# Rotary embedding on split heads: all transfers on one queue in one fixed order

## The chip, the cores and the metric

The kernel runs on one core of a Trainium2 chip. The metric is device time in microseconds (us); the time before is the median of three runs. Times inside the run are from one profiled execution and count from its first instruction. Sizes such as 2048 KB are in units of 1024 bytes, as the profile gives them; MB and GB/s are decimal.

## What is computed

Each of 16 heads of 64 elements is rotated by tables `cos` and `sin` that depend on the position in the sequence:

```python
batch, seq, dim = (16, 512, 1024)      # float32, num_heads = 16
x = x.reshape(batch, seq, num_heads, head_dim)
x1, x2 = (x[..., :half_dim], x[..., half_dim:])
cos = cos[None, :, None, :]; sin = sin[None, :, None, :]
rotated = np.concatenate([x1 * cos - x2 * sin, x1 * sin + x2 * cos], axis=-1)
```

So 33.55 MB are read and 33.55 MB are written. All arithmetic is in float32.

## The kernel before

**Tiles.** Each batch is 512 rows of 1024 values, which is 4 rows on each of 128 partitions (2048 KB). The first two and the last two batches are moved one at a time (single tiles, 2048 KB); the twelve between them are moved as six pairs (pair tiles, 4096 KB, 8 rows to a partition). That makes ten tiles: 0 and 1 single, 2 to 7 pairs, 8 and 9 single. This text calls the load of tile t Lt and its store St. A "row" below is one 128x1024 piece, so there are 64 of them.

**The ring.** `x_sb` holds 40 rows. The work is done in place: a tile is loaded into the ring, its rows are overwritten by the results, and the store reads from there. Tiles 0 to 5 fill the ring. Tile 6 takes the place of tiles 0 and 1, tile 7 that of tile 2, tiles 8 and 9 that of tile 3; so L6 must wait until S0 and S1 have landed, L7 until S2, and L8 and L9 until S3 (`sem_out`).

**Compute.** For a row, VectorE multiplies by cos into PSUM (`t1_ps`, L293), and GpSimd multiplies the swapped halves by the signed sin table into `t2_sb` (L257); for one row of each pair tile VectorE does that second product as well (L286). The two products are added by VectorE (L304, 43 rows), or by TensorE with an identity matrix into the same PSUM (L224), after which ScalarE copies the sum to the ring (L191, 21 rows). There are three PSUM buffers and six `t2_sb` buffers, so the engines can run apart by a few rows only. At the start ScalarE and TensorE also lay out the tables for the pair tiles.

**Transfers.** Two hardware queues are used, one for each direction. ScalarE issues the loads and the two 64 KB table transfers (L153, L174): L0, the tables, and L1 to L5 at once at the start, which fill the ring; the other four loads stand between its copies, `LAG` = 10 rows after the last row of what they overwrite, and each first waits on `sem_out`. SyncE issues the stores (L161), each as soon as the last row of its tile is added (`wait_added`). On SyncE nothing else is queued. The end of the kernel is SyncE's wait on `sem_rest` for the last stores (L162).

The order of the engines' own work is written out by hand and is the same before and after; nothing in it is decided by a scheduler.

Of the kernel before, what the change touches and what calls it, by code (L numbers as in the profile page):

```python
# [6 lines left out]
def bass_split_heads_rope_kernel(  # L7
# [21 lines left out]
    R1 = seq // P  # L29
    R2 = 2 * R1  # L30
# [10 lines left out]
    tiles = [(b, R1 if b in singles else R2) for b in range(batch) if b in singles or b % 2 == 0]  # L41
    NT = len(tiles)
    RING = 5 * R2

    rows = [(t, r) for t, (_, n) in enumerate(tiles) for r in range(n)]
    NU = len(rows)
    EARLY = (NU - RING) // R2


    V_ROW = 3  # L50
    PE2 = [R1 <= u < NU - R1 and u % R2 in (1, 3, 6) for u in range(NU)]
# [11 lines left out]
    BANK = 512  # L63
    EH = H * HD // BANK
    LEAD = 1
    LAG = 10

    with ExitStack() as stack:
        x_sb = stack.enter_context(nc.sbuf_tensor([P, RING, H, 2, HALF], fp32))
        t2_sb = stack.enter_context(nc.sbuf_tensor([P, NT2, H, 2, HALF], fp32))  # L70
        stage = stack.enter_context(nc.sbuf_tensor([P, 2, R1 * HALF], fp32))
# [9 lines left out]
        sem_out = [stack.enter_context(nc.semaphore(f"out{k}")) for k in range(EARLY)]  # L81
        sem_rest = stack.enter_context(nc.semaphore("rest"))
        sem_cos = stack.enter_context(nc.semaphore("cos"))
        sem_sin = stack.enter_context(nc.semaphore("sin"))
# [28 lines left out]
        def in_dram(single, pairs, t):  # L113
            b, n = tiles[t]
            return single[b] if n == R1 else pairs[:, b:b + 2, :]

        def in_sbuf(t):
            b, n = tiles[t]
            k = b * R1 % RING
            return x_sb[:, k:k + n].rearrange("p n h t d -> p (n h t d)")  # L120

        def where(u):
            t, r = rows[u]
            return t, r, u % RING
# [7 lines left out]
        def wait_added(eng, u):  # L132

            if n_pe[u]:
                eng.wait_ge(sem_a, n_pe[u])
            if n_comb[u]:
                eng.wait_ge(sem_v, n_comb[u])
# [10 lines left out]
        def stores_of(k):  # L148

            return sum(b * R1 // R2 == k for b, _ in tiles)  # L150

        def load(eng, t):
            eng.dma_start(in_sbuf(t), in_dram(x1, x2, t)).then_inc(sem_in[t], 16)  # L153

        def on_sync(sp):
            for u in range(NU):
                t, r, k = where(u)
                if r == tiles[t][1] - 1:
                    wait_added(sp, u)
                    k = u // R2  # L160
                    sp.dma_start(in_dram(o1, o2, t), in_sbuf(t)).then_inc(sem_out[k] if k < EARLY else sem_rest, 16)  # L161
            sp.wait_ge(sem_rest, 16 * sum(stores_of(k) for k in range(EARLY, NU // R2)))  # L162

        def on_scalar(ae):
            later = {}
            for t, (b, n) in enumerate(tiles):
                if b * R1 + n <= RING:
                    load(ae, t)
                else:

                    later.setdefault((b * R1 - RING) // R2 * R2 + R2 - 1 + LAG, []).append(t)
                if t == 0:
                    for i, (table, sem) in enumerate(((cos, sem_cos), (sin, sem_sin))):
                        ae.dma_start(stage[:, i, :], table.rearrange("(s r) d -> s (r d)", r=R1)).then_inc(sem, 16)  # L174

            ae.wait_ge(sem_i, 2)
            ae.activation(  # L177
                pick[:], ident[:].rearrange("q (s k) -> q k s", k=2)[:, :, :, None].broadcast_to([P, 2, P // 2, 2]), COPY
            ).then_inc(sem_g, 1)
            ae.wait_ge(sem_sin, 16)  # L180
            sv = stage[:, 1, :].rearrange("s (r d) -> s r d", d=HALF)
            ae.activation(s1_sb[:, :, 0, :], sv, COPY, scale=-1.0)  # L182
            ae.activation(s1_sb[:, :, 1, :], sv, COPY).then_inc(sem_s, 1)  # L183
            ae.wait_ge(sem_t, 2)
            s2 = s2_sb[:].rearrange("p (k r) t d -> p k r t d", r=R1)
            ae.activation(s2[:, :, :, 0, :], pair_ps[:, :, 1, :, :], COPY, scale=-1.0)  # L186
            ae.activation(s2[:, :, :, 1, :], pair_ps[:, :, 1, :, :], COPY).then_inc(sem_s, 1)  # L187
            for u in range(NU):
                if PE2[u]:
                    ae.wait_ge(sem_e, n_pe[u])  # L190
                    ae.activation(xs[:, u % RING, :], t1_ps[:, u % NT1, :], COPY).then_inc(sem_a, 1)  # L191
                for t in later.get(u, ()):
                    k = (tiles[t][0] * R1 - RING) // R2
                    ae.wait_ge(sem_out[k], 16 * stores_of(k))
                    load(ae, t)

        def on_tensor(pe):
            pe.wait_ge(sem_z, 1)
# [62 lines left out]
        def on_vector(ve):  # L261
# [49 lines left out]
            for u in range(NU + LEAD):  # L311
                if u < NU:
                    mul(u)
                if u >= LEAD and not PE2[u - LEAD]:
                    comb(u - LEAD)

        on_sync(nc.sync)
        on_scalar(nc.scalar)
        on_gpsimd(nc.gpsimd)
        on_tensor(nc.tensor)  # L320
# [34 lines left out]
```

## Time and profile before

| What | Before |
|---|---|
| Time, median of 3 runs (lowest to highest) | 161.23 us (161.17 to 161.33) |
| Profiled execution: span, first to last instruction | 160.3 us |
| GpSimd busy | 134.9 us (84%) |
| VectorE busy | 130.3 us (81%) |
| TensorE busy | 72.8 us (45%) |
| ScalarE busy | 24.4 us (15%) |
| Moved | 67.26 MB, mean 419 GB/s |
| Transfers | 10 loads, 10 stores, 2 tables |

How to read it: the page gives the profiled execution its span alone and no second time of its own, so the span stands for it. The median of the runs is 0.9 us more than the span; that part lies before the first or after the last instruction of the profile. Busy times add up instructions on one engine and say nothing about which wait ends last. A transfer's "time to landing" runs from its issue to the moment when its semaphore is complete, so it holds the time in which it was queued behind others.

### The profile page before, as it was taken

Reading aid. Unit: us, or ns where it says so; the run is one execution under the profiler, and the core shown is the slowest. Engines: PE = TensorE matmul, PEld = TensorE weight load, DVE = VectorE, ACT = ScalarE, POOL = GpSimd, SP = SyncE. Lnnn points to the kernel's source line nnn. Section 1 sums busy time; section 2 is a strip of 40 time slices with the busy share of each in tenths; the row PEclk is TensorE's granted clock in tenths of the full one; section 3 lists DMA queues with packets and bytes.
Section 4 is the critical chain, followed back from the end, with each engine's and each line's share of the span. In section 5 each row is a group of like instructions: output and inputs, shape, how many; then the busy total and the mean of one; then the engine's idle time right before and its main releaser. Section 6 shows DMA issues by size and latency. Waiting matters only on the chain.

```text
span 160.3 us, 522 instructions
## 1 busy us (share of the span) xinstructions
PE 72.8 (45%) x94; PEld 24.0 (15%) x94; DVE 130.3 (81%) x117; ACT 24.4 (15%) x27; POOL 134.9 (84%) x64
## 2 busy tenths in 40 slices
PE   6050004478357936660847105489458435850000
PEld 1020002022202211210221002022202111220000
DVE  0069998599989999996999709899889999999500
ACT  0420000203120222022012010201220402040000
POOL 1059999999999999999999999699999999289400
PEclk9955555557755587689687965555555977699555
DMA  5999999999999999999999999999999999999896
GB/s 147 409 441 474 409 450 409 425 429 429 446 429 458 417 411 466 409 433 401 450 433 425 425 409 458 409 433 433 411 429 462 441 417 401 450 441 441 376 450 294
DMA packets 3170, 67.26 MB, mean 419 GB/s; under 512 B 352, under 2 KB 608, under 8 KB 608
## 3 DMA queue, kind: packets, MB, share of 16 engines
q10 hardware_dynamic: 1728, 33.69, 49.6%
q1 hardware_dynamic: 1440, 33.56, 48.9%
q14 instruction: 2, 0.02, 0.0%
HBM read 33.69 MB, written 33.55 MB: 419 GB/s over the span
## 4 chain that ended last, share of the span: by engine, by line
DMA 60%; POOL 13%; DVE 8%; PE 7%; issue 3%; ACT 2%; ACTq 1%; DVEq 0%
DMA x_sb<-in_x_dram 41%; DMA out_dram<-x_sb 18%; POOL t_sb L257 13%; PE t_ps L224 7%; DVE t_ps L293 5%; DVE x_sb L304 3%; ACT x_sb L191 2%; ACTq L153 1%; ACTq L174 1%; DVE t_sb L286 0%; DVEq L303 0%
## 5 line engine op out<-in xcount | busy, mean ns | idle before, releaser
L257 POOL TENSOR_TENSOR t_sb<-x_sb,s_sb 128x1024 f32<-128x1024 f32 x58 | 134.2, 2346 | 14.8 <-ACT s_sb L183 8.5
L224 PE MATMUL t_ps<-t_sb,ident 128*128 128x512 f32 x84 | 68.0, 957 | 63.0 <-DVE t_ps L293 39.2
L293 DVE TENSOR_TENSOR t_ps<-x_sb,pair_ps 128x1024 f32<-128x1024 f32 x48 | 57.7, 1223 | 9.9 <-ACT x_sb L191 9.8
L304 DVE TENSOR_TENSOR x_sb<-t_ps,t_sb 128x1024 f32<-128x1024 f32 x43 | 52.4, 1218 | 2.6 <-POOL t_sb L257 2.6
L224 PEld LDWEIGHTS t_ps<-t_sb,ident 128*128 128x128 f32 x84 | 22.1, 290 | 108.9 <-DVE t_ps L293 74.6
L191 ACT ACTIVATE x_sb<-t_ps 128x1024 f32<-128x1024 f32 x21 | 21.5, 1023 | 109.9 <-PE t_ps L224 96.9
L293 DVE TENSOR_TENSOR t_ps<-x_sb,tab_ps 128x1024 f32<-128x1024 f32 x16 | 19.3, 1222 | 0.1
L286 DVE TENSOR_TENSOR t_sb<-x_sb,tab_ps 128x1024 f32<-128x1024 f32 x6 | 7.3, 1213 | 0.0
L264 DVE COPY tab_ps<-stage 128x128 f32<-128x128 f32 x1 | 0.3, 294 | 7.8 <-DMA stage<-in_cos_dram 7.8
L208 PE MATMUL pair_ps<-stage,pick 128*128 128x256 f32 x4 | 2.0, 667 | 5.4 <-DMA stage<-in_sin_dram 5.4
L201 PE MATMUL t_ps<-zero 128*128 128x512 bf16 x6 | 2.7, 627 | 1.3 <-DVE zero L262 1.3
L208 PEld LDWEIGHTS pair_ps<-stage,pick 128*128 128x128 f32 x4 | 1.2, 324 | 6.4 <-issue 6.3
L177 ACT ACT_TABLE_LOAD x1 | 1.3, 1283 | 5.5 <-issue 5.5
L201 PEld LDWEIGHTS t_ps<-zero 128*128 128x128 bf16 x6 | 0.7, 136 | 2.4 <-DVE zero L262 1.2
L262 DVE MEMSET zero<- 128x256 uint32 x1 | 0.3, 272 | 0.9 <-PEq L337 0.9
L186 ACT ACTIVATE s_sb<-pair_ps 128x256 f32<-128x256 f32 x1 | 0.4, 383 | 1.7 <-PE pair_ps L208 1.7
L182 ACT ACTIVATE s_sb<-stage 128x128 f32<-128x128 f32 x1 | 0.3, 309 | 2.1 <-DMA stage<-in_sin_dram 2.1
L235 POOL MEMSET ident<- 128x128 f32 x1 | 0.2, 204 | 0.3 <-POOLq L337 0.3
L177 ACT ACTIVATE pick<-ident 128x256 f32<-128x256 f32 x1 | 0.4, 416 | 0.0
L187 ACT ACTIVATE s_sb<-pair_ps 128x256 f32<-128x256 f32 x1 | 0.4, 379 | 0.0
L237 POOL TENSOR_SCALAR_AFFINE_SELECT ident<-ident 128x128 f32<-128x128 f32 x1 | 0.3, 292 | 0.1
L337 POOL MEMSET const-float32-0.0<- 128x1 f32 x1 | 0.1, 98 | 0.3 <-issue 0.3
(6 smaller groups left out, 1.0 us busy)
## 6 DMA issues: line engine op xcount, KB each, us to landing
x_sb<-in_x_dram ACTq DMA_DIRECT2D x6, 4096.0 KB, 38.0
out_dram<-x_sb SPq DMA_DIRECT2D x6, 4096.0 KB, 25.0
x_sb<-in_x_dram ACTq DMA_DIRECT2D x4, 2048.0 KB, 22.6
out_dram<-x_sb SPq DMA_DIRECT2D x4, 2048.0 KB, 15.2
stage<-in_cos_dram ACTq DMA_DIRECT2D x1, 64.0 KB, 7.8
stage<-in_sin_dram ACTq DMA_DIRECT2D x1, 64.0 KB, 7.5
```

The lines of the kernel that those rows point to most:

```text
L153: eng.dma_start(in_sbuf(t), in_dram(x1, x2, t)).then_inc(sem_in[t], 16)
L174: ae.dma_start(stage[:, i, :], table.rearrange("(s r) d -> s (r d)", r=R1)).then_inc(sem, 16)
L177: ae.activation(pick[:], ident[:].rearrange("q (s k) -> q k s", k=2)[:, :, :, None].broadcast_to([P, 2, P // 2, 2]), COPY).then_inc(sem_g, 1)
L186: ae.activation(s2[:, :, :, 0, :], pair_ps[:, :, 1, :, :], COPY, scale=-1.0)
L191: ae.activation(xs[:, u % RING, :], t1_ps[:, u % NT1, :], COPY).then_inc(sem_a, 1)
L201: pe.matmul(t1_ps[:, k, b * BANK:(b + 1) * BANK], zero[:, 0:P], zero[:], start=True, stop=True).then_inc(sem_w, 1)
L208: pe.matmul(pair_ps[:, k].rearrange("p c r d -> p (c r d)"), pick[:, k].rearrange("q s b -> q (s b)"), stage[:].rearrange("q c f -> q (c f)"),
L224: ins = pe.matmul(t1_ps[:, u % NT1, b * BANK:(b + 1) * BANK], ident[:], t2[:, b * BANK:(b + 1) * BANK], start=False, stop=True, skip_group ...
L257: pl.tensor_tensor(t2_sb[:, u % NT2, :, :, :], swapped(k), over_heads(s_of(t, r)), mult).then_inc(sem_p, 1)
L286: ve.tensor_tensor(t2_sb[:, u % NT2, :, :, :], swapped(k), over_heads(v_ps), mult)
L293: ve.tensor_tensor(t1_ps[:, u % NT1, :].rearrange("p (h d) -> p h d", d=HALF), x_sb[:, k, :, :, :].rearrange("p h t d -> p (h t) d"), c_of ...
L304: ve.tensor_tensor(xs[:, k, :], t1_ps[:, u % NT1, :], t2_sb[:, u % NT2, :, :, :].rearrange("p h t d -> p (h t d)"), add,).then_inc(sem_v, 1)
```

## The change

All transfers move to SyncE's queue. A list `ORDER`, written out by hand, gives their order: L0, both tables, L1, L2, L3; S0, S1; L4, L5; S2; L6; S3; L7; S4; L8, L9; S5 to S9. SyncE walks down the list: before a load that reuses ring space it waits on `sem_out`, before a store it waits until the tile's last row is added, and then it issues. ScalarE issues no transfer and no longer waits on `sem_out`; `LAG` and the table of later loads are gone. Which ring rows and semaphores are used, the shapes of the transfers, and the instructions of VectorE, GpSimd, TensorE and ScalarE's arithmetic and their order stay as they were.

```diff
+    ORDER = [("load", 0), ("table", 0), ("table", 1)]
+    for kind, which in (
+        ("load", (1, 2, 3)),
+        ("store", (0, 1)),
+        ("load", (4, 5)),
+        ("store", (2,)),
+        ("load", (6,)),
+        ("store", (3,)),
+        ("load", (7,)),
+        ("store", (4,)),
+        ("load", (8, 9)),
+        ("store", (5, 6, 7, 8, 9)),
+    ):
+        ORDER += [(kind, t) for t in which]
...
-    LAG = 10
...
         def on_sync(sp):
-            for u in range(NU):
-                t, r, k = where(u)
-                if r == tiles[t][1] - 1:
-                    wait_added(sp, u)
-                    k = u // R2
+            for kind, t in ORDER:
+                b, n = tiles[t]
+                k = b * R1 // R2
+                if kind == "table":
+                    table, sem = ((cos, sem_cos), (sin, sem_sin))[t]
+                    sp.dma_start(stage[:, t, :], table.rearrange("(s r) d -> s (r d)", r=R1)).then_inc(sem, 16)
+                elif kind == "load":
+                    if b * R1 + n > RING:
+                        free = (b * R1 - RING) // R2
+                        sp.wait_ge(sem_out[free], 16 * stores_of(free))
+                    load(sp, t)
+                else:
+                    wait_added(sp, b * R1 + n - 1)
                     sp.dma_start(in_dram(o1, o2, t), in_sbuf(t)).then_inc(sem_out[k] if k < EARLY else sem_rest, 16)
...
         def on_scalar(ae):
-            later = {}
-            for t, (b, n) in enumerate(tiles):
-                if b * R1 + n <= RING:
-                    load(ae, t)
-                else:
-
-                    later.setdefault((b * R1 - RING) // R2 * R2 + R2 - 1 + LAG, []).append(t)
-                if t == 0:
-                    for i, (table, sem) in enumerate(((cos, sem_cos), (sin, sem_sin))):
-                        ae.dma_start(stage[:, i, :], table.rearrange("(s r) d -> s (r d)", r=R1)).then_inc(sem, 16)
-
...
-                for t in later.get(u, ()):
-                    k = (tiles[t][0] * R1 - RING) // R2
-                    ae.wait_ge(sem_out[k], 16 * stores_of(k))
-                    load(ae, t)
```

More of the change, by code (lines that the diff above doesn't have):

```diff
@@ L47, in bass_split_heads_rope_kernel @@
     EARLY = (NU - RING) // R2
+    ORDER = [("load", 0), ("table", 0), ("table", 1)]
[12 more added lines that the diff above has]
+        ORDER += [(kind, t) for t in which]
+    assert NT == 10
     V_ROW = 3
```

## The prediction

> **What bounds the kernel now.** I read the page's engine shares first, then the DMA slices and queues, then the chain that ended last.
>
> ```profile
> PE 72.8 (45%) x94; PEld 24.0 (15%) x94; DVE 130.3 (81%) x117; ACT 24.4 (15%) x27; POOL 134.9 (84%) x64
> ...
> DMA  5999999999999999999999999999999999999896
> ...
> q10 hardware_dynamic: 1728, 33.69, 49.6%
> q1 hardware_dynamic: 1440, 33.56, 48.9%
> ```
>
> No engine reaches 85%, but the two DMA queues (q10 the loads, q1 the stores) hold the 16 DMA engines for 49.6 + 48.9 = 98.5% of the span, and no slice between the first and the last three is under 9. The transfers are the bound from end to end. The chain hides this: it names a late load and then compute.
>
> ```profile
> 93.45 47.51 DMA x_sb<-in_x_dram
> ...
> 141.02 9.29 POOL t_sb L257 x4
> ...
> 150.40 1.23 DVE x_sb L304
> ```
>
> Here GpSimd waits for L9 until 140.96 and S9 is issued at 151.70. But S8 lands only at 143.56 + 11.9 = 155.5, and S9 4.8 us later, which is just the time of 2048 KB (below). The queue was full when S9 arrived, so making this compute tail earlier brings nothing by itself.
>
> How fast do the queues go? Single issues, asked from the trace one by one, with the time to landing last; in order L1, L2, S7, S8, S9:
>
> ```profile
> x_sb<-in_x_dram ACTq DMA_DIRECT2D x1, 2048.0 KB, 11.9
> x_sb<-in_x_dram ACTq DMA_DIRECT2D x1, 4096.0 KB, 20.9
> out_dram<-x_sb SPq DMA_DIRECT2D x1, 4096.0 KB, 15.1
> out_dram<-x_sb SPq DMA_DIRECT2D x1, 2048.0 KB, 11.9
> out_dram<-x_sb SPq DMA_DIRECT2D x1, 2048.0 KB, 8.6
> ```
>
> Their issues start at 2.17, 2.87, 135.58, 143.56 and 151.70 us, so they land at 14.05, 23.76, 150.64, 155.5 and 160.3 (unrounded landings where rounding matters).
>
> - **Loads alone:** L2 lands 9.71 us after L1, for 4096 KB.
> - **Stores alone:** S9 lands 9.66 us after S7, also 4096 KB (S8 and S9).
> - **Both directions:** between L2's landing and S7's, 126.88 us, lie L3 to L9 (24 MiB) and S0 to S7 (28 MiB), thirteen units of 4096 KB: 9.76 each.
>
> At the one-way prices these thirteen would take 6 x 9.71 + 7 x 9.66 = 125.9 us. So running side by side costs about 1.0 us in all. The trace's packet records agree: a 32 KB packet takes 1,213 ns in both one-way stretches without exception worth counting; in the two-way stretch most still take 1,213, but some take up to 1,571. The excess over 1,213 (611 for 16 KB), summed between 22 and 140 us and divided by 16 engines, is 0.96 us.
>
> **The change part by part.**
>
> *Loads and stores in blocks.* In the new order the queue is first in, first out, so the data time is: L2's landing at 23.76, as before, since L0, the tables, L1 and L2 keep their order and nothing runs beside them; then 58.3 us for six units of loads, 67.6 us for seven units of stores, and 9.66 for S8 and S9. That is 159.3 us. Not all of the 1.0 us is won: the 16 engines drift apart (one transfer's engines finish up to 2.7 us apart in the records), so around each of the nine changes of direction both kinds still run together for some 2 us, 18 us of the 117 that are two-way now. 18/117 of 1.0 is 0.16; I give back 0.2. Bounds of this part: 0 (the excess isn't due to the mixing) to -1.0; I take -0.8, because both one-way rows, 21 and 17 us long, show no excess.
>
> *Changes of direction in one queue.* The trace of before never shows a load behind a store in the same queue. Lower bound 0: the packets of the two queues alternate on each engine, and if I join each packet's end to the next start, about 800 changes each way have a mean gap of -3 ns; transfers joined in one queue (L1 to L2, S8 to S9) show none either. Upper bound: where a load follows a store, its opening latency is exposed, 1.0 us (L0: issued at 0.81, first packet at 1.82), at most 3.1 (L0's landing after 8.0 us less 4.86 of data). I take 0, since the nearest row, the same engine turning round between two packets, is nearly the case itself. A page speaks against it: the Trainium skill, "DMA: Bandwidth & Descriptors", section "Latency and other measured facts", gives an HBM access 2 us under high load; four loads that start behind a store would by that make the time 8 us longer, an estimate from that page which no row here supports.
>
> *Stores queued behind loads.* No store now competes with loads issued before it, but each must be issued before the queue runs dry. By the sum, the queue comes to the stores at these times (landing of the transfer ahead), against the issue times of before: S0 33.5 against 20.5, S1 38.3 against 31.0, S2 62.5 against 47.5, S3 81.9 against 63.7, S4 101.3 against 81.1, S5 120.7 against 102.7, S6 130.4 against 119.6, S7 140.0 against 135.6, S8 149.7 against 143.6, S9 154.5 against 151.7. S9 was issued 3.8 us ahead of S8's landing without harm, so about 4 us of lead are needed. All have it but S9 with 2.8; and S9 was held by GpSimd's wait for L9, which now lands at 120.7 instead of 141.0. These rows show what goes:
>
> ```profile
> POOL t_sb L257 <- DMA x_sb<-in_x_dram: 4.3, 2, 3.9
> ...
> ACT x_sb L191 <- issue: 8.9, 1, 8.9
> ```
>
> The 3.9 us of the first row were that wait; without it S9 goes out at about 147.8, a lead of 6.7.
>
> *SyncE's waits.* Behind each wait on SyncE stand all later transfers. L6 stands behind S2's wait, so it goes out at 47.5 and is due at 72.2. L7 waits for S2's landing at 72.2 and is due at 91.6; L8 waits for S3's at 91.6 and is due at 111.0. Each has 19 us or more. S4 behind L7's wait is free at 72.2 and not ready before 81. Twelve issues move to SyncE at 0.3 to 0.6 us each, while a 2048 KB transfer takes 4.8: hidden under the queue's backlog.
>
> *Loads for compute.* GpSimd works without a gap from 9.85 to 99.94 us, seven rows to a pair tile, 2.31 each: it comes to tiles 3, 4, 5, 6 at about 45, 61, 77, 93. L3 to L6 land at 33.5, 52.8, 62.5 and 81.9. L4 has 8 us, the least.
>
> *ScalarE issues none.* The 8.9 us of the last row are ScalarE standing in `sem_out` before L8; VectorE waited 5.3 us for it at 91 to 97 us. Both go. Priced at nothing, since the queue hides it; it adds to the stores' leads above. At the start L0 goes out on SyncE rather than ScalarE, after the same opening, so no change.
>
> *The rule on queues.* The Trainium skill, the same page, section "Issuing engines are not separate DMA queues", says that transfers from all issuing engines share the same 16 DMA engines and that spreading them saves only issue time. By this rule alone one queue and two would come to the same time, 161.2; the rows above put 1.0 us on the mixing itself.
>
> *Sum.* Span 160.3 - 1.0 + 0.2 = 159.5. The runs' median stands 0.9 above the span: 160.4 us.
>
> **The rivals.**
>
> 1. *Blocks save most of the mixing cost* (the forecast): 160.4. Own range 159.9 to 160.9: all of the 1.0 and the last engines' spread (the last store's engines end over 1.2 us, some of which the slow packets made) on one side, a third of it on the other. Chance 0.58.
> 2. *The excess isn't due to the mixing* but to the chip's memory or to transfers being set up; then it stays, and the time is 161.2. For it: it comes in bursts (22 to 30, 72 to 78, 92 to 96, 124 us), near issues, and 30 to 52 us, mixed throughout, shows hardly any. Against: none in the one-way stretches. Chance 0.2.
> 3. *A load behind a store pays for turning round* (slower). Place: S1 to L4, S2 to L6, S3 to L7, S4 to L8. At 1.0 us each, 160.4 + 4.0 = 164.4; at 3.1 each, 172.8. Above 0.2 us each it eats the gain, above 0.28 it is measurably slower; at 0.7 each the time is 163.2. Against it stand the gapless alternations; for it only that no row shows it inside one queue. Chance 0.17.
> 4. *A store comes late and the queue runs dry* (slower). It would be S7, whose lead is the smallest without help, 4.4 us. If compute slipped by 2 us and 4 of lead are needed, 1.6 are lost: 162.0. Against: two known stalls vanish. Chance 0.05.
>
> **How the numbers follow.** The two-way excess is small, so even the best case is only 0.7% off. A difference of 0.2%, 0.3 us, is about what can be told from no change here. Rival 1 gives faster, nearly all of it, plus a little of rival 2's spread: 0.6. Rival 2 with the low end of rival 1 gives same: 0.2. Rivals 3 and 4 give slower: 0.2. The range runs from 159.8, just under the forecast's own, to 162.6, which takes in rivals 2, 4 and turning costs up to 0.55 us each; what it leaves out is the dearer part of rival 3 (about 0.12) and a few in a hundred below.
>
> **What would show it.** Right: the sums of queue shares near 98.5% again with one queue alone, L9 landing near 121 instead of 141, one-way and two-way packets all at 1,213 ns, 9.7 us for each 4096 KB wherever one looks, S9's issue near 148, and the chain made of transfers. Wrong: DMA slices under 9 at the changes of direction (rival 3), or just ahead of a store's issue (rival 4); packets above 1,213 ns in blocks of one direction (rival 2). It would also fall if loads now arrived late, seen as new GpSimd waits for a load.

## The result, and the profile after

The changed kernel is slower: 163.25 us, median of four runs (163.02 to 163.45), against 161.22 before (161.17 to 161.33). The ratio is 1.012, with a 95% interval of 1.0106 to 1.0133. The forecast was 160.4 us with a range of 159.8 to 162.6, so both the sign and the range were missed.

The page of the changed kernel, span, DMA slices and queue:

```profile
span 161.6 us, 522 instructions
...
DMA  5999999999999999999999999999999999999993
...
q1 hardware_dynamic: 3168, 67.24, 97.8%
```

One queue now carries everything, and no slice in the middle is under 9. The packet records show no gap at the changes of direction either: on each of the 16 engines the next transfer's first packet starts where the last one ended (within 4 ns at all nine changes). The end differs: the last three slices are 9, 9, 3 where before had 8, 9, 6. The chain and SyncE's own waits in the changed kernel:

```profile
POOL 68%; DMA 11%; issue 8%; SPq 1%; DVE 1%; DVEq 0%
...
SPq L184 <- DMA out_dram<-x_sb: 16.0, 1, 16.0
```

The chain now names GpSimd for 68% of the span, and again it misleads. The second line says why: after the last store is issued, SyncE waits 16.0 us for it to land. GpSimd's timeline in the changed kernel:

```profile
9.76 134.03 POOL L264 TENSOR_TENSOR t_sb<-x_sb,s_sb 128x1024 f32<-128x1024 f32 x58 [8.39 <-ACT s_sb L194]
```

All its rows run as one block and end at 143.8. The compute side became better, as forecast: S9 is issued at 145.2 instead of 151.7. That was worth nothing, since the queue ahead of it was full.

Where the time goes shows in single transfers. Time to landing of L2, L3, S2, L6, S3 and L7 in the changed kernel, each from its own issue:

```profile
x_sb<-in_x_dram SPq DMA_DIRECT2D x1, 4096.0 KB, 20.7
x_sb<-in_x_dram SPq DMA_DIRECT2D x1, 4096.0 KB, 30.1
out_dram<-x_sb SPq DMA_DIRECT2D x1, 4096.0 KB, 25.8
x_sb<-in_x_dram SPq DMA_DIRECT2D x1, 4096.0 KB, 35.3
out_dram<-x_sb SPq DMA_DIRECT2D x1, 4096.0 KB, 29.7
x_sb<-in_x_dram SPq DMA_DIRECT2D x1, 4096.0 KB, 30.4
```

Their issues start at 3.00, 3.71, 47.11, 47.77, 63.12 and 72.93 us. So L3 lands 10.1 us after L2, L6 10.2 after S2, L7 10.5 after S3: three loads with a store behind them take 0.4 to 0.8 us more than the 9.71 of a load with a load behind it. (L5 and L9, which have a store behind them too, do not: 9.7 for the 4096 KB of L5 after L4, and 4.8 for the 2048 KB of L9 after L8.) A landing is that of the last of 16 engines. The packet records show the first one too, by the semaphore write with which each engine ends its share. This text calls the time between the first and the last engine's write for one transfer the *spread*:

| End of transfer | Before, first engine | Spread | After, first engine | Spread |
|---|---|---|---|---|
| L1 | 12.8 | 0.81 | 12.6 | 0.84 |
| S2 | 71.3 | 1.80 | 71.4 | 1.04 |
| L6 | 89.3 | 2.17 | 81.1 | 1.64 |
| L7 | 108.8 | 2.15 | 100.5 | 2.56 |
| S7 | 149.0 | 1.21 | 148.9 | 2.56 |
| S9 | 158.7 | 1.21 | 158.6 | 2.56 |

The fastest engine ends S9 at the same time in both kernels, within 0.1 us. The spread is 1.35 us larger in the changed one, gained for the most part in steps at L6 and L7, and its slowest engine ends S9 1.27 us later (161.21 against 159.94), which is the difference of the two spans, 1.3 us. The last stretch, in windows of the changed kernel and then of the kernel before (window and length, then the busy time of each engine, the granted clock, DMA share, GB/s), shows it on the DMA side:

```profile
158.60:161.20 2.60, 0.00 (x0) 0.00 (x0) 0.00 (x0) 0.00 (x0) 0.00 (x0) 0.50 0.21 88
```

```profile
158.70:160.00 1.30, 0.00 (x0) 0.00 (x0) 0.00 (x0) 0.00 (x0) 0.00 (x0) 0.50 0.30 126
```

For 2.6 us at the end, most of the 16 DMA engines have finished (share 0.21) and the store waits for a few; before, that lasted 1.3 us.

### The profile page after: what moved, and what is told of

It reads as the page before. It is cut to its first block, busy times and chain, and to the rows that moved or that the text cites. A ratio compares the mean times of both kernels' runs of the same rounds, so it can differ in the third digit from the quotient of the medians.

```text
span 161.6 us, 522 instructions
## 1 busy us (share of the span) xinstructions
PE 70.2 (43%) x94; PEld 23.3 (14%) x94; DVE 129.9 (80%) x117; ACT 24.4 (15%) x27; POOL 134.7 (83%) x64
## 3 DMA queue, kind: packets, MB, share of 16 engines
q1 hardware_dynamic: 3168, 67.24, 97.8%
## 4 chain that ended last, share of the span: by engine, by line
POOL 68%; DMA 11%; issue 8%; SPq 1%; DVE 1%; DVEq 0%
POOL t_sb L264 68%; DMA x_sb<-in_x_dram 11%; DVE x_sb L311 1%; SPq L167 1%; SPq L175 1%; DVEq L310 0%
## 5 line engine op out<-in xcount | busy, mean ns | idle before, releaser
L231 PE MATMUL t_ps<-t_sb,ident 128*128 128x512 f32 x84 | 65.4, 928 | 60.0 <-POOL t_sb L264 39.2
L300 DVE TENSOR_TENSOR t_ps<-x_sb,pair_ps 128x1024 f32<-128x1024 f32 x48 | 57.6, 1222 | 2.7 <-ACT x_sb L202 2.4
L231 PEld LDWEIGHTS t_ps<-t_sb,ident 128*128 128x128 f32 x84 | 21.4, 282 | 103.9 <-DVE t_ps L300 57.0
L293 DVE TENSOR_TENSOR t_sb<-x_sb,tab_ps 128x1024 f32<-128x1024 f32 x6 | 7.3, 1213 | 0.0
```

The lines of the kernel that those rows point to most:

```text
L231: ins = pe.matmul(t1_ps[:, u % NT1, b * BANK:(b + 1) * BANK], ident[:], t2[:, b * BANK:(b + 1) * BANK], start=False, stop=True, skip_group ...
L293: ve.tensor_tensor(t2_sb[:, u % NT2, :, :, :], swapped(k), over_heads(v_ps), mult)
L300: ve.tensor_tensor(t1_ps[:, u % NT1, :].rearrange("p (h d) -> p h d", d=HALF), x_sb[:, k, :, :, :].rearrange("p h t d -> p (h t) d"), c_of ...
```

## The experiments

The theories at the start: **A**, each place in a queue where a store stands behind a load (or each change of direction) costs time, and the 16 engines pay unevenly, so that the last one falls behind; **B**, one queue in place of two is the cause whatever the order in it. "Places" below counts the places where a store follows a load in the same queue without a gap. The changed kernel has five: L3 to S0, L5 to S2, L6 to S3, L7 to S4, L9 to S5.

### Two places, and seven

The order alone is changed. Two places:

```diff
-        ("load", (1, 2, 3)),
-        ("store", (0, 1)),
-        ("load", (4, 5)),
-        ("store", (2,)),
-        ("load", (6,)),
-        ("store", (3,)),
-        ("load", (7,)),
-        ("store", (4,)),
-        ("load", (8, 9)),
-        ("store", (5, 6, 7, 8, 9)),
+        ("load", (1, 2, 3, 4, 5)),
+        ("store", (0, 1, 2, 3)),
+        ("load", (6, 7, 8, 9)),
+        ("store", (4, 5, 6, 7, 8, 9)),
```

> Same single queue, but only 3 changes of direction instead of 9 (L0 to L5, S0 to S3, L6 to L9, S4 to S9). In the changed kernel the last store's engines end 2.6 us apart (1.2 before), while the first engine ends as early as before. Theory A, each change of direction in one queue makes some engines lose time: the span loses about 1.26/9 = 0.14 us per change, so 6 fewer changes give a span near 160.8 and a time near 162.3. Theory B, one queue instead of two is the cause whatever the order: span 161.6, time 163.2. In either case the time stands 1.4 us above the span if that larger distance belongs to the single queue.

Measured: 161.42 us beside 161.42 before, ratio 1.0001 [0.9991, 1.0011]. The page of this kernel, span, DMA slices and queue:

```profile
span 160.2 us, 522 instructions
...
DMA  5999999999999999999999999999999999999996
...
q1 hardware_dynamic: 3168, 67.24, 98.3%
```

The same single queue with the same bytes costs nothing when it changes direction three times instead of nine. Theory B falls. The number that A was given, an even price for each change (span 160.8, time 162.3), was missed as well: the time fell below it. Seven places:

```diff
         ("load", (1, 2, 3)),
-        ("store", (0, 1)),
-        ("load", (4, 5)),
+        ("store", (0,)),
+        ("load", (4,)),
+        ("store", (1,)),
+        ("load", (5,)),
         ("store", (2,)),
         ("load", (6,)),
...
         ("load", (7,)),
         ("store", (4,)),
-        ("load", (8, 9)),
-        ("store", (5, 6, 7, 8, 9)),
+        ("load", (8,)),
+        ("store", (5,)),
+        ("load", (9,)),
+        ("store", (6, 7, 8, 9)),
```

> Same single queue, 13 changes of direction instead of 9: stores and loads alternate one by one from S0 to L9. Theory A (a price per change): span 161.6 + 4 x 0.14 = 162.2, time about 163.8. Theory B (the single queue whatever the order): span 161.6, time 163.2.

Measured: 163.83 us (one of its four runs 162.58), ratio 1.0135 [1.0095, 1.0175]. DMA slices of its page:

```profile
DMA  5999998999999999999999999998999999999991
```

The last slice is down to 1 tenth: the spread of S9 is 3.51 us. This is what A expected.

### Three places, and two again

```diff
-        ("load", (1, 2, 3)),
-        ("store", (0, 1)),
-        ("load", (4, 5)),
-        ("store", (2,)),
-        ("load", (6,)),
-        ("store", (3,)),
-        ("load", (7,)),
-        ("store", (4,)),
+        ("load", (1, 2, 3, 4, 5)),
+        ("store", (0, 1, 2)),
+        ("load", (6, 7)),
+        ("store", (3, 4)),
         ("load", (8, 9)),
         ("store", (5, 6, 7, 8, 9)),
```

> Single queue with three places where a store follows a load (L0 to L5, S0 to S2, L6, L7, S3, S4, L8, L9, S5 to S9). From two such places to seven the spread of the engines grew, between L1 and the end, by 0.74, 1.72 and 1.83 (five places), 3.05 us: 0.35 to 0.44 a place. Theory A therefore expects 1.1 to 1.3 us of growth here, a span of 160.2 to 161.0, between the two on either side. A theory without a price per place (only the first change of direction counts, or only the single queue) expects the value of the kernel with two places (160.0) or that with five (161.0 to 162.0).

Measured: 162.43 us, ratio 1.0065 [1.0046, 1.0085]; spans 160.7 to 161.2, between the neighbours on either side. The spread grew by only 0.75 us between L1 and S9 in its profile, less than the 1.1 to 1.3 expected.

> The kernel with two places where a store follows a load, again, on the same chip as the one with three. Span 159.9 to 160.2, as in its first run; the last store's engines 1.0 to 1.3 us apart.

Measured beside it: 161.53 us, ratio 0.9999 [0.9971, 1.0026]. The profiled execution was one of its longer ones (span 160.7, the others 159.9 to 160.4); it began with a spread of 1.23 at L1, and S9 had 1.77, outside the 1.0 to 1.3 expected.

### The changed kernel again

> The changed kernel as it is, for a second profile and beside the others on one chip. Theory A (a price for each of the five places where a store follows a load in the queue, paid unevenly by the 16 engines): spans of 161.0 to 162.0 again, the last store's engines over 2 us apart, steps in that spread at places where a store follows a load, and the records of the last load packet before such a place above 1,213 ns, those before a load that follows a store at 1,213. Theory B (the single queue whatever its order) expects the spread to grow evenly along the run.

Measured: 162.81 us, ratio 1.0098 [1.0076, 1.0121], spans 161.0 to 161.9. In its profile the spread is 0.85 to 0.97 us up to L4 and steps up at L5 (1.16), L6 (1.60), L7 (2.18) and L9 (2.78). Each of these is a load with a store behind it; through the transfers between them and the five stores at the end it stays level. So the growth comes in steps at the places that A names, and not evenly. L6 and L7 step up in both profiles, L5 and L9 in this one alone.

### Gaps before the stores, and gaps before the loads

First, a store that follows a load is issued only when that load has landed:

```diff
-            for kind, t in ORDER:
+            for i, (kind, t) in enumerate(ORDER):
+                last = ORDER[i - 1]
...
+                    if last[0] == "load":
+                        sp.wait_ge(sem_in[last[1]], 16)
                     wait_added(sp, b * R1 + n - 1)
```

> The changed kernel, but each store that follows a load in the list is issued only once that load has landed, so that no store is queued behind a load in flight. If the queued store stretches the load's last packets (theory A), all load packets take 1,213 ns, the spread of the engines stays near 1 us, and the time is the five drained changes alone: about 1.3 us from last data to landing and 1.0 to 3 from issue to first packet, 2.5 to 4 each, a span of 172 to 180. If the stretch has nothing to do with the store behind it, it stays at the same places and the span is higher still by 1 us.

Measured: 175.35 us, span 173.9, both from a single run. The loads ahead of the gaps were not lengthened, as expected; that the last packets of the stores ahead of loads were, on all engines, was not (table below). Then the mirror, a load that follows a store is issued only when that store has landed:

```diff
+        land = {4: stack.enter_context(nc.semaphore("land4"))}
...
-            for kind, t in ORDER:
+            for i, (kind, t) in enumerate(ORDER):
+                last = ORDER[i - 1]
...
+                    if i and last[0] == "store":
+                        v = last[1]
+                        j = tiles[v][0] * R1 // R2
+                        sp.wait_ge(land[v], 16) if v in land else sp.wait_ge(sem_out[j], 16 * stores_of(j))
                     load(sp, t)
...
-                    sp.dma_start(in_dram(o1, o2, t), in_sbuf(t)).then_inc(sem_out[k] if k < EARLY else sem_rest, 16)
-            sp.wait_ge(sem_rest, 16 * sum(stores_of(k) for k in range(EARLY, NU // R2)))
+                    sp.dma_start(in_dram(o1, o2, t), in_sbuf(t)).then_inc(sem_out[k] if k < EARLY else land.get(t, sem_rest), 16)
+            sp.wait_ge(sem_rest, 16 * (sum(stores_of(k) for k in range(EARLY, NU // R2)) - len(land)))
```

> The mirror of the kernel whose stores wait for the load ahead: here each load that follows a store in the list is issued only once that store has landed (four places), and stores follow loads directly. With the stores drained, the last packets before each load were stretched on all 16 engines, 540 to 710 ns on average, and those before each store not at all. If the first change of direction after the engines have started in step is what all of them pay for, the last load packets before S2, S3, S4 and S5 are now stretched by 300 to 700 ns on average (1 to 77 in the changed kernel), and those before the drained loads not at all. If a change from load to store is cheap on average except the first of the run, they stay under 100. Span 161.8 + 4 x 2.5 to 4, 172 to 178.

Measured: 179.94 us, span 178.5, again one run. Both times are dominated by the gaps, as meant; the DMA slices of the first and the second kernel show them:

```profile
DMA  6999989499999957899959999399896899998998
```

```profile
DMA  5999999895998999948999599898599999999996
```

What they tell is in the packet records. For each change, the mean over 16 engines of what the last packet before the change took above 1,213 ns (611 for 16 KB), in ns:

| Change | As changed | Gap before stores | Gap before loads |
|---|---|---|---|
| L3 to S0 | 348 | 6 (gap) | 472 |
| L5 to S2 | 6 | 1 (gap) | 818 |
| L6 to S3 | 77 | 0 (gap) | 930 |
| L7 to S4 | 66 | 0 (gap) | 844 |
| L9 to S5 | 1 | 0 (gap) | 162 |
| S1 to L4 | 1 | 541 | 0 (gap) |
| S2 to L6 | 27 | 713 | 0 (gap) |
| S3 to L7 | 14 | 706 | 0 (gap) |
| S4 to L8 | 1 | 681 | 0 (gap) |

This is the clearest result. The packets that are lengthened are those just ahead of a direct change of direction, the last one above all. The one before it is lengthened on single engines in the changed kernel, and on average by 0.61 to 0.67 us at L5, L6 and L7 of the mirror kernel, which the table does not hold. The first change after the queue has stood empty is paid for by nearly all engines, 0.2 to 0.9 us on average, and in either direction. Later changes in a queue that keeps running cost little on average, and only those from load to store cost much on single engines: in the last packet up to 586 ns before S3 and 318 before S4 in the changed kernel, where the largest before a load is 176, and in the packet before the last up to 974 before S4. Two of these packets make the two large steps: the engine that ends L6 last had the 586, and the engine that ends L7 last had the 974. The average expected for the mirror kernel, 300 to 700, was too low in three places and too high in one.

### A small load in between

```diff
+            last, count_small = "", [0]
...
                     load(sp, t)
+                    last = kind
                 else:
+                    if last == "load":
+                        sp.dma_start(spare[:, count_small[0], :], sin.rearrange("(s r) d -> s (r d)", r=R1)).then_inc(sem_small, 16)
+                        count_small[0] += 1
+                    last = kind
```

> The changed kernel with one more 64 KB load (the sin table, into a buffer that nobody reads) between each load and the store that follows it, five in all, 0.15 to 0.25 us each by the table transfers at the start, 1.0 us in all. If the large load packet in flight is what is stretched by a store behind it, the small packets take its place and the spread goes: span 160.0 + 1.0 = 161.0. If it is the change of direction as such, it stays: 161.8 + 1.0 = 162.8.

Measured: 163.92 us, ratio 1.017 [1.0149, 1.0190], span 162.3 to 162.9. S9's spread is 2.59 us, grown by 1.87 since L1, as without the small loads. The small packets did not take the place of the large ones. All 640 of them took at most 29 ns, and the last large load packets were lengthened as before, though eight packets of 512 bytes now stood on each engine between them and the store: up to 692 ns ahead of S0 and of S4, and 309 ahead of S3. Keeping a store some 0.2 us away from the load does not help; the change of direction keeps its price. (The time is 1.1 us over the changed kernel's 162.81 beside it, about what five more loads were expected to add.)

### Parts of the change back on ScalarE's queue

The later loads back on ScalarE, with `LAG` as before; SyncE keeps L0 to L5, the tables and all stores.

```diff
         ("store", (0, 1)),
         ("load", (4, 5)),
-        ("store", (2,)),
-        ("load", (6,)),
-        ("store", (3,)),
-        ("load", (7,)),
-        ("store", (4,)),
-        ("load", (8, 9)),
-        ("store", (5, 6, 7, 8, 9)),
+        ("store", (2, 3, 4, 5, 6, 7, 8, 9)),
...
+    LAG = 10
...
+            later = {}
+            for t, (b, n) in enumerate(tiles):
+                if b * R1 + n > RING:
+                    later.setdefault((b * R1 - RING) // R2 * R2 + R2 - 1 + LAG, []).append(t)
...
+                for t in later.get(u, ()):
+                    k = (tiles[t][0] * R1 - RING) // R2
+                    ae.wait_ge(sem_out[k], 16 * stores_of(k))
+                    load(ae, t)
```

> SyncE issues L0 to L5, the tables and all stores in blocks (S0 and S1 before L4 and L5); L6 to L9 go back to ScalarE's queue, as before, so that loads and stores run side by side in two queues from about 54 us on. If the stretch with the single queue from 70 us on makes the engines drift apart (the steps in the changed kernel stand at L6 and L7): the last store's engines end about 1.2 us apart, span 160.3 to 160.5. If the drift comes from the start: span 161.6. The distance of time and span is 0.9 us if using ScalarE's queue at all decides it, 1.4 us if not.

Measured: 162.85 us (161.69 to 163.03), ratio 1.0068 [1.0036, 1.0100]. It does not separate the two. The DMA slices of its page, and a window of it:

```profile
DMA  5999999999999999999999999999999999699997
```

```profile
139.00:141.50 2.50, 0.17 (x1) 0.17 (x2) 2.09 (x3) 1.01 (x1) 2.50 (x2) 0.50 0.58 249
```

S7 was issued at 140.0, when the queue had run dry (S6's first engine ends at 139.2); the DMA share falls to 0.58 and S9's spread is 0.15, because all engines waited. ScalarE stands again in its wait on `sem_out`, 13.7 us at the longest, and holds up compute. It shows how small the margin of the stores is, not what the queues cost.

The early loads back on ScalarE (L0, tables, L1 to L5 at the start); the rest on SyncE in the changed order. Three places are left.

```diff
-    ORDER = [("load", 0), ("table", 0), ("table", 1)]
+    ORDER = []
     for kind, which in (
-        ("load", (1, 2, 3)),
-        ("store", (0, 1)),
-        ("load", (4, 5)),
-        ("store", (2,)),
+        ("store", (0, 1, 2)),
         ("load", (6,)),
         ("store", (3,)),
...
         def on_scalar(ae):
+            load(ae, 0)
...
+            for t in range(1, 6):
+                load(ae, t)
```

> ScalarE's queue takes L0 to L5 and the tables at the start, as before; all else stays on SyncE in the changed order, so that S0, S1, S2 run beside L3 to L5 in two queues and only three places are left where a store follows a load in one queue (L6 to S3, L7 to S4, L9 to S5). Theory A: 159.9 + 3 x 0.36 = 161.0 in span, 162.4 in time. If the side-by-side start repairs the spread as in the kernel before, or if only the first change of direction in the one queue costs, 160.0 and 161.4.

Measured: 162.46 us, ratio 1.0083 [1.0053, 1.0113]; spread 1.00 us at L1 and 1.94 at S9, stepping at L7 (1.22), L8 (1.65) and L9 (1.94). The same loss as the single queue with three places (162.43). So the price per place is there with the early loads in the other queue too. The step at L8 does not fit A: behind L8 stands a load, and the lengthened packet (424 ns over 611) is the third one after a change from store to load.

The tables alone on ScalarE:

```diff
-    ORDER = [("load", 0), ("table", 0), ("table", 1)]
+    ORDER = [("load", 0)]
...
         def on_scalar(ae):
+            for i, (table, sem) in enumerate(((cos, sem_cos), (sin, sem_sin))):
+                ae.dma_start(stage[:, i, :], table.rearrange("(s r) d -> s (r d)", r=R1)).then_inc(sem, 16)
```

> The changed kernel with the two 64 KB table transfers issued by ScalarE. Span as changed, 161.6 (within 0.3), as the order of the large transfers is the same. The time stands 1.4 us above the span in the changed kernel and 0.9 before: if a kernel that uses both queues has the smaller distance, this one shows 0.9 and a time of 162.5; if the distance goes with SyncE's number of transfers, 1.4 and 163.0.

Measured: 162.69 us (162.11 to 164.53), ratio 1.0105 [1.0068, 1.0142]. The distance of time and span is 1.4 us here, and it turned out to be 1.4 (1.37 to 1.49) in every run on record with both numbers, the runs of the kernel before included. There is no second loss outside the span. The profiled execution of before, with its span of 160.3, was simply one of its longer ones: 21 runs of that kernel beside these have spans of 159.7 to 160.3 and a median of 160.0. (Of the 50 beside all the experiments three were longer: 160.9, 161.9 and 163.1. A single execution of the kernel before can be as long as one of the changed kernel.) In this kernel's profile the whole set of engines paid at L5 to S2 (packets started between 60 and 62 us hold 0.57 us of excess per engine), which in the changed kernel cost 6 ns: the price of one place is not the same from run to run. Here the loss is not one of spread: S9's is 1.31 us, only 0.83 more than L1's, but the first engine ends S9 at 159.4 instead of 158.6, and the excess after 13 us is 1.56 us per engine instead of 0.92. (The sine table lands with L1, and GpSimd's first multiplication waits 13.3 us instead of 8.4; no slice in the middle is under 9, so the queue hides that.)

### Two queues, and no store behind a load in flight

ScalarE issues L0 to L5 and later S4 to S9, between its copies; SyncE issues S0 to S3, from L4's landing on, and L6 to L9.

```diff
+    ORDER = []
     for kind, which in (
...
+        ("store", (0, 1, 2, 3)),
+        ("load", (6, 7, 8, 9)),
...
+                    if t == 0:
+                        sp.wait_ge(sem_in[4], 16)
                     wait_added(sp, b * R1 + n - 1)
...
         def on_scalar(ae):
+            load(ae, 0)
...
+            for t in range(1, 6):
+                load(ae, t)
+            last_row = {4: 43, 5: 43, 6: 49, 7: 57, 8: NU - 1, 9: NU - 1}
...
+                for t in sorted(last_row):
+                    if last_row[t] == u:
+                        store(ae, t)
```

> Two queues again, each with at most one change of direction from store to load and none from load to store while data is flowing: ScalarE issues L0 to L5 and later, between its copies, S4 to S9; SyncE issues S0 to S3 (S0 after L4 has landed) and then L6 to L9. Loads and stores run side by side only at the two ends of the load stretches. Theory A: no place at which a queued store stretches a load in its own queue, so span 159.7 to 160.2 and a time at or below that of before. If mixing itself costs as the prediction held, the gain over before is up to 0.7 us; if the queue runs dry because ScalarE issues late, it shows as slices under 9 near 110 us and a span over 161.

Measured: 161.54 us, ratio 1.0020 [1.0010, 1.0029], span 159.9 to 160.5. Span and queues of its page:

```profile
span 160.0 us, 523 instructions
```

```profile
q10 hardware_dynamic: 2016, 42.08, 61.8%
q1 hardware_dynamic: 1152, 25.17, 36.6%
```

The spread grows from 0.91 (L1) to 1.06 us (S9) only, as A expects, but the kernel is no faster than before. The excess of the packets after 13 us is down to 0.58 us per engine, from 0.96 in the profile of before. This profile's span is 0.3 us shorter than that one, but that one was a longer execution by as much; by the medians nothing of the 0.38 is gained. No version tried beats the kernel before.

### All of it in one table

Each time is a median, each ratio is to runs of the kernel before taken beside it, and each spread is that of one profiled execution. The two kernels with gaps, 175.35 and 179.94 us, are left out.

| Kernel | Places | Time, us | Ratio to before | Spread at L1, at S9 |
|---|---|---|---|---|
| Two queues, split | 0 | 161.54 | 1.0020 | 0.91, 1.06 |
| Single queue | 2 | 161.42, 161.53 | 1.0001, 0.9999 | 0.43, 1.17 and 1.23, 1.77 |
| Single queue | 3 | 162.43 | 1.0065 | 1.04, 1.79 |
| Early loads on ScalarE | 3 | 162.46 | 1.0083 | 1.00, 1.94 |
| Later loads on ScalarE (queue ran dry) | 2 | 162.85 | 1.0068 | 0.99, 0.15 |
| As changed | 5 | 163.25, 162.81 | 1.012, 1.0098 | 0.84, 2.56 and 0.95, 2.78 |
| Small load in between | 5 | 163.92 | 1.0170 | 0.72, 2.59 |
| Tables on ScalarE | 5 | 162.69 | 1.0105 | 0.48, 1.31 |
| Single queue | 7 | 163.83 | 1.0135 | 0.46, 3.51 |

In the single queue, from two places to seven, the time rises by 163.83 - 161.42 = 2.4 us, about 0.5 for each added place, though not on a straight line, and the spread at the end rises with it. The kernel with the tables on ScalarE fits by its time but not by its spread: its loss lies on all engines. So the time goes with the number of places, and whether a few engines pay or all of them differs from run to run.

## Why the prediction was wrong

**The step that failed first is "Changes of direction in one queue", taken at 0.** The sum put the price as a gap between packets, bounded it by the opening latency of a load, and found alternating packets of two queues without a gap. There is indeed no gap. The price is in the length of the last packet before the change, and two queues that alternate all the time do not show it. The same engine turning round between packets of two queues was taken for nearly the case itself, and it was not. In the changed kernel one engine's packets were lengthened by 0.59 us at L6 and 0.97 at L7, nothing made that up, and S9 ended 1.27 us later than before. Rival 3 had the right family, with a chance of 0.17, but the wrong place: it put the price on loads behind stores. In the changed kernel's running queue those cost 1 to 27 ns on average; stores behind loads are what the time goes with. That its 163.2 us at 0.7 each is nearly the measured 163.25 is a coincidence.

**The second is the gain from blocks, -0.8 us.** The excess of 1.0 us side by side was read rightly, but it is a mean over engines. With the blocks the mean stayed where it was (0.92 us after 13 us, from 0.96), 0.35 of it at the first change alone, which all engines pay. In the two-place kernel (0.63 and 0.57) and in the split kernel (0.58) it was 0.33 to 0.39 us less, and the median time did not follow. What ends the kernel is the last of 16 engines, and the sum had no term for the spread beyond a remark in the range. Together the first two steps make the miss in the profiled span, 161.6 against 159.5: 0.8 us not won and 1.3 us of lag.

**The third is the 0.9 us between span and median.** It joined a longer execution's span to the median of other runs, and so was too small for the part of the time outside the profile, which it was taken for. With the 1.4 us that all runs show, the forecast would have been 159.5 + 1.4 = 160.9, and the kernel before 161.7 in that execution.

**What held.** The issue times and leads: S9 went out at 145.2 (about 147.8 was expected), all stores had their lead, and GpSimd's waits for loads and ScalarE's stand in `sem_out` went. L9 landed at 122.8 instead of 141.0, 2 us later than the sum's 120.7. The share of the queue fell only to 97.8%, and the slices stayed at 9. The sign that the prediction named for rival 3, slices under 9 at the changes, did not appear although a price of turning round was paid: one engine in sixteen that loses 0.6 us takes 1% of a slice of 4 us. Packets above 1,213 ns in blocks were the sign that did appear.

The Trainium skill ("DMA: Bandwidth & Descriptors", section "Issuing engines are not separate DMA queues") holds that one queue or two differ in issue time alone. That agrees with the two-place kernel (1.0001) and not with the changed one (1.012): the number of queues cost nothing here, the order within the one did. Of the 2 us that the same page gives for an HBM access under load, 8 us in all by the estimate, nothing was seen: in the changed kernel the last store packet ahead of a load was 1 to 27 ns over 1,213 (611) on average, with no gap behind it.

**What stays open.** Why the packet ahead of a change is lengthened, at the memory, in the DMA engine or between them, is not shown. Nor is why the first change after an empty queue is paid for by all engines and later ones by a few, or which ones. Of the 0.92 us of excess per engine in the changed kernel 0.54 lies on the last packets of transfers and 0.17 on the ones before them; the rest lies on single packets elsewhere, such as one of 551 ns in the middle of L5, and is not explained. That the last engine's lag makes the difference is shown for the two profiled executions, 1.27 us; the medians differ by 2.0, because the profiled execution of before was a longer one (161.7 by its span, median 161.22) and that of the changed kernel a shorter one (163.02, median 163.25). In other runs the loss can lie on all engines, as the kernel with the tables on ScalarE shows.

## What to carry to other kernels

In a kernel bound by its transfers, the end is set by the slowest of the 16 DMA engines: look at the spread of the engines' last writes, not only at the busy share or the mean packet, before pricing a gain in tenths of a microsecond. If loads and stores share one queue, change direction as seldom as the buffers allow; beyond two, each place where a store stood behind a load cost about 0.5 us here. And take the distance between span and time from runs that have both.

## What the runs showed of the hardware

- The last packet before a direct change from load to store, or the reverse, can take longer than the 1,213 ns of a 32 KB packet: by 0.54 to 0.93 us on average over 16 engines at the first change after a gap (0.16 where the packets were 16 KB before S5), and later in the changed kernel by up to 0.6 us on single engines, with up to 0.97 in the packet before it. In the kernel with the tables on ScalarE, L5 to S2 cost 0.57 on average without a gap ahead of it.
- Two queues with one direction each alternate packet by packet at a mean excess of about 10 ns a packet (mean 1,223 against 1,213). The mean in the changed kernel is no higher (1,222), but there it lies on a few packets of a few engines.
- An engine's lag was not made up in the changed kernel: the spread of 2.56 us from L7 on stands unchanged in every transfer until S9. In other kernels with a single queue it did shrink by up to 0.3 us where the engines ahead paid at a change, as from 1.04 to 0.77 us at L5 with three places.
- Draining a queue before a change cost 12 to 17 us for five and four changes (spans 173.9 and 178.5 against 161.6), 2.5 to 4.2 each.
